# A two-layer decoder trunk on one core: c spread from a column, the compression MLP's matrices in long runs, the last sums ended in turn, and an order chosen with other durations

## The chip, the core and the metric

The kernel runs on one core of one Trainium2 chip. The metric is device time in microseconds (us), the median of several executions; a profiled execution of the same program shows where the time lies. The engines in the profile: PE is TensorE (matmuls; PEld its weight loads), DVE is VectorE, ACT is ScalarE, POOL is GpSimd, SP is SyncE, whose queue (SPq) issues nearly all loads. The engines work through their own instruction streams in order and wait for each other by semaphores.

## The reference, cut to what matters

```python
def reference(x, c, positions, w_ada, b_ada, norm_mix, norm_ffn, w_in, ...):
    cos, sin = rope_angles(positions)
    for l in range(DEPTH):
        ada = jax.nn.silu(c) @ w_ada[l] + b_ada[l]
        sh_m, sc_m, g_m, sh_f, sc_f, g_f = jnp.split(ada[:, None, :], 6, axis=-1)
        h = rms_norm(x, norm_mix[l]) * (1.0 + sc_m) + sh_m
        (q_a, kc_a, vc_a, ..., q_b, k_b, v_b, g_br) = jnp.split(h @ w_in[l], split_at, axis=-1)
        y_a = nsa_mixer(...)     # k_c = gelu(blocks(kc_a) @ ck_w1) @ ck_w2, likewise v_c
        y_b = moba_mixer(...)
        gate_a, gate_b = jnp.split(jax.nn.sigmoid(g_br), 2, axis=-1)
        merged = gate_a * (y_a @ w_up_nsa[l]) + gate_b * (y_b @ w_up_moba[l])
        x = x + g_m * (merged @ w_out[l])
        h = rms_norm(x, norm_ffn[l]) * (1.0 + sc_f) + sh_f
        gt, up = jnp.split(h @ w_ffn_in[l], 2, axis=-1)
        x = x + g_f * ((jax.nn.silu(gt) * up) @ w_ffn_out[l])
    return x
```

There are two layers, x is 256 tokens by 1024, c is one vector of 1024, and the hidden width of the second sublayer is 2816. All of it is float32. `nsa_cmp_k_w1` and `nsa_cmp_v_w1` (here ck_w1, cv_w1) are 2048 by 128.

## The kernel before

The 256 tokens are two tiles of 128 rows (t = 0, 1). A weight matrix is read once, in units of 1 MB (128 partitions by 2048 floats, a tile called raw; the first pass over w_in has units of 128 by 1816). To keep float32's precision at a faster matmul format, ACT rounds a unit to a tile hi, DVE forms lo = raw - hi, and PE does three matmuls for each product: hi with the activation's hi part, lo with it, and hi with the activation's lo part (hp holds both parts of h, hd is h before the split). A few units are multiplied as float32 straight from raw. There are three raw slots (and one spare), a few hi and lo slots, three slots aw for parts of w_ada, and eight banks for sums.

The kernel begins with a **lead**: x and c come in, silu(c) is spread over all partitions as crow (128 by 1024), and for each k of 8 the loads are a pair, sa (the shift and scale parts of w_ada, 1 MB) and raw (w_in). `ada_dot` (L707) multiplies sa by crow and sums each row on DVE; that gives the modulation of h for block k, without which hd and hp of that block, and so PE's matmuls on that unit, can't begin. In the lead POOL and ACT also work out the rotary tables (sincos, ct, st). c comes as a row of 1 by 1024 on SP's queue, ahead of x; two matmuls of a tile `ones` (1 by 128) with the row spread it.

After the lead comes the rest of w_in in units raw<-in_w_in. At its start stands the compression MLP (`mlp`, L1232), on the two matrices w1: each is loaded into a raw slot as 128 partitions by 16 pieces of 128 floats. Its 64 small matmuls need e, which DVE builds from the first products; `at` is ACT's copy of what they give, and two matmuls with `sel` follow. Further on are attention, w_up, w_out, then w_ffn_in and w_ffn_out (`sublayer_ffn`, L1538), and the second layer in the same way. Parts of w_ada for later use come in 0.5 MB pieces (aw) among the weight units, each with one ada_dot on DVE.

At the end, the last units of w_ffn_out end four sums (t, c), each a bank of 128 by 512. `gate` spreads g_f by eight transposes of gcol and two copies (gbc); `resid` (L1528) multiplies each bank by gbc and adds it to x on DVE, and SP stores the piece.

**What sets the order.** The code only records operations. `Program.order` (L246) then goes through them as a list scheduler with a duration for each operation, latencies between engines, and a model of the DMA queue, gives out slots and banks, and fixes each engine's stream. `levels` (L220) ranks operations by the longest path behind them; a `boost` is added to the rank. `fill` (L401) puts matmuls of zeros (zb) into PE's idle stretches longer than 1.4 us of the plan. `blame` and `rounds` (L421, L439) repeat the plan with other boosts and keep the shortest. So a changed duration can move any instruction on any engine.

Of the kernel before, what the change touches and what calls it, by code (L numbers as in the profile page):

```python
# [16 lines left out]
P = 128  # L17
# [107 lines left out]
LOOSE = {}  # L125
# [6 lines left out]
class Program:  # L132
    WAIT = 1.0

    FILL, IDLE, ZERO = 1.4, 1.0, 0.23
    FIRST_ZERO = (0.43, 11)

    ROUNDS, WEIGHT, START = 40, 1.0, 15.0
# [81 lines left out]
    def levels(self):  # L220
# [15 lines left out]
        for op in reversed(self.ops):  # L236
            c = min(c for c, _ in op.alts.values()) + (op.bytes / 385e3 + 2.0 if op.bytes else 0.0)
# [8 lines left out]
    def order(self):  # L246
# [17 lines left out]
        free = {e: 0.0 for e in LAT}  # L264
# [7 lines left out]

        def place(op):
            t = 0.0
            taken = {}
            picks = []
            if any(not v.placed for v in op.acc if v not in op.new):
                return None
            for v in op.new:
# [3 lines left out]
                if len(k.queue) <= i or k.queue[i] is not v:  # L283

                    if sum(not c.busy for s in k.slots for c in s.cells) - i <= LOOSE.get(v.name, 99):
                        return None
# [20 lines left out]
        while left:  # L307
            left -= 1
            best = None
            per = {}  # L310
            while loads and loads[0] in issued:
                loads.popleft()
            for op in ready:
# [5 lines left out]
                for e, (c, _) in op.alts.items():  # L319
# [4 lines left out]
                    per.setdefault(e, []).append((est, op, pl[1], c))  # L324
            self.done, self.ready = out, ready
            assert per, "stuck"
            for e, cs in per.items():
                t0 = min(c[0] for c in cs)
                if e == "SP":
                    pick = min(cs, key=lambda c: (max(c[0], free[e] + 0.3), c[1].no))  # L330
                else:
                    w = eps[e] + (self.SWITCH if e == "PE" else 0.0)
                    pick = max((c for c in cs if c[0] <= t0 + w), key=lambda c: (c[1].rank(e), -c[1].no))
                    if pick[3] > 1.0 and e != "PE":

                        soon = [c for c in cs if c[0] < t0 + self.WAIT * pick[3]
                                and c[1].rank(e) > pick[1].rank(e) + 5.0]
                        if soon:
                            pick = min(soon, key=lambda c: (c[0], -c[1].rank(e)))
                if best is None or pick[0] < best[0]:  # L340
                    best = (pick[0], e, pick[1], pick[2], pick[3])
            t, e, op, picks, c = best
            if len(op.alts) > 1:

                done = {x: next(y[0] for y in per[x] if y[1] is op) + op.alts[x][0] for x in op.alts}
                e = min(done, key=lambda x: done[x] + self.BIAS.get(x, 0.0))
                c = op.alts[e][0]
                t = done[e] - c
# [3 lines left out]
            for v, s in zip(op.new, picks):  # L352
                v.kind.queue.remove(v)
                v.slot, v.placed = s, True
                for cell in s.cells:
# [14 lines left out]
            if op.bytes:  # L370
                free[e] = t + c
                if e == "SP":
                    dma = max(dma, t + c + 0.5) + op.bytes / 385e3
                    end = dma + 2.0
                else:
                    end = t + c + 6.5
# [24 lines left out]
    def fill(self, t0, t1):  # L401
# [5 lines left out]
        cost, n = self.ZERO, int((t1 - t0 - self.IDLE) / self.ZERO)  # L407
        if t0 < 3.0:
            cost, n = self.FIRST_ZERO
# [29 lines left out]
    def rounds(self):  # L439

        best = None
        for i in range(self.ROUNDS):
# [4 lines left out]
            for op in self.ops:  # L447
                op.boost += self.WEIGHT * to.get(op.no, 0.0)
# [12 lines left out]
class Engines:  # L461
# [12 lines left out]
    def _vec(self, engs, n, two, fn, reads, writes, psum=False, extra=0.0):  # L474
        alts = {}
        for e in engs:
# [3 lines left out]
            else:  # L480
                alts[e] = (0.3 + n * (2.7e-3 if two else 2.0e-3) + extra, [lambda: fn(self.nc.gpsimd)])
# [89 lines left out]

SPILL = [("kb",), ("kb",)]
# [14 lines left out]
def trunk_kernel(tc, pools, A):  # L587
# [77 lines left out]
    ones = const("ones", [1, P])  # L665
# [302 lines left out]
    def consts():  # L968
# [5 lines left out]
        pool_memset(ones, 1.0, "DVE")  # L974
# [693 lines left out]
```

## Time and profile before

| | us |
|---|---|
| median of 3 runs | 835.67 (834.61 to 836.22) |
| the profiled execution, its own time | 833.42 |
| its span in the trace | 831.5 |
| PE busy | 810.5 (97%) |
| DVE busy | 578.0 (70%) |
| ACT busy | 419.9 (50%) |
| POOL busy | 66.1 (8%) |

The span runs from the first instruction to the end of the last, and 1.9 us of the execution's time lie outside it. Busy PE counts matmuls of zeros too. The granted clock over the span was 0.994 of the full one.

### The profile page before, as it was taken

To read this page: it belongs to the slowest core of one execution; us is meant where nothing else is said; L and a number is where in the kernel's file an instruction comes from. 1 tells how busy PE (TensorE), PEld (TensorE's weight loads), DVE (VectorE), ACT (ScalarE), POOL (GpSimd) and SP (SyncE) were. 2 spreads that over 40 slices of the span, in tenths; PEclk is the share of its full clock that TensorE was granted. 3 is DMA by queue.
4 is the path that set the end of the run, shared out by engine and by line. 5 is a ranking of instruction groups with operands and counts; after the bars stand their busy time and mean duration, and the time that the engine had idled before them with its cause. 6 is when DMAs were issued, how large, how long until landed. Compare 5 with 4: busy or idle time off the path is not lost.

```text
span 831.5 us, 10528 instructions
## 1 busy us (share of the span) xinstructions
PE 810.5 (97%) x3983; PEld 612.0 (74%) x3983; DVE 578.0 (70%) x1014; ACT 419.9 (50%) x667; POOL 66.1 (8%) x69
## 2 busy tenths in 40 slices
PE   9998999999999999999999999999999999999996
PEld 4566756764768887898878877776567888889885
DVE  6878877777787776778778897866378534464443
ACT  6444465861583433444376556587457534443331
POOL 4602610000000000000000313000000000000000
PEclk9999999999999999999999999999999999999999
DMA  9987474449938899887948775540284455465531
GB/s 364 381 302 254 135 263 134 178 158 333 343 121 298 281 304 327 303 308 287 347 153 283 248 239 183 187 151 1 102 294 162 138 189 181 151 203 202 200 104 50
DMA packets 75252, 183.82 MB, mean 221 GB/s; under 512 B 4129, under 2 KB 9265, under 8 KB 75202
## 3 DMA queue, kind: packets, MB, share of 16 engines
q1 hardware_dynamic: 75154, 183.08, 62.9%
q8 instruction: 31, 0.51, 0.3%
q14 instruction: 19, 0.16, 0.1%
q0 software_dynamic: 48, 0.08, 0.0%
HBM read 182.10 MB, written 1.05 MB: 220 GB/s over the span
## 4 chain that ended last, share of the span: by engine, by line
PE 77%; DVE 8%; DMA 8%; ACT 3%; issue 2%; POOL 2%; SPq 0%; DVEq 0%; POOLq 0%; ACTq 0%
PE bank L550 72%; PE bank L555 5%; DVE lo L485 4%; DMA aw<-in_w_ada 2%; DMA raw<-in_w_in 2%; ACT hi L533 2%; DMA rows<-in_rows 1%; DVE tmp L485 1%; DMA raw<-in_w_ffn_in 1%; DMA raw<-in_w_out 1%; POOL tmp L485 1%; DVE tmp L503 1%; POOL tmp L503 1%; DVE aw L491 1%; ACT hp L533 1%
## 5 line engine op out<-in xcount | busy, mean ns | idle before, releaser
L550 PE MATMUL bank<-hi,hp 128*128 128x512 f32 (+2 forms) x1296 | 408.8, 388 | 1.5 <-DVE hp L485 0.7
L485 DVE TENSOR_TENSOR lo<-raw,hi 128x2048 fp32r<-128x2048 f32 (+2 forms) x107 | 243.0, 2286 | 122.6 <-ACT hi L533 122.4
L533 ACT ACTIVATE hi<-raw 128x2048 fp32r<-128x2048 f32 (+2 forms) x107 | 201.7, 1892 | 230.3 <-PE bank L550 173.3
L550 PEld LDWEIGHTS bank<-hi,hp 128*128 128x128 f32 x1296 | 239.3, 189 | 57.0 <-issue 6.5
L550 PE MATMUL bank<-lo,hp 128*128 128x512 f32 (+2 forms) x648 | 244.9, 378 | 4.2 <-DVE lo L485 4.0
L550 PEld LDWEIGHTS bank<-lo,hp 128*128 128x128 f32 x648 | 122.4, 189 | 29.7 <-DVE lo L485 6.9
L491 DVE SCALAR_TENSOR_TENSOR aw<-aw,crow 128x1024 f32<-128x1024 f32 x80 | 95.8, 1219 | 24.6 <-DMA aw<-in_w_ada 24.4
L550 PE MATMUL bank<-hi,aT 128*128 128x512 f32 x352 | 111.9, 392 | 0.0
L550 PEld LDWEIGHTS bank<-hi,aT 128*128 128x128 f32 x352 | 66.1, 188 | 13.4
L550 PE MATMUL bank<-lo,aT 128*128 128x512 f32 x176 | 68.6, 390 | 0.0
L550 PE MATMUL bank<-raw,yy 128*128 128x512 f32 x128 | 58.3, 598 | 0.1
L550 PE MATMUL bank<-raw,hd 128*128 128x512 f32 (+1 forms) x112 | 49.1, 568 | 0.0
L550 PE MATMUL bank<-hi,mT 128*128 128x512 f32 x128 | 43.2, 404 | 0.1
L550 PEld LDWEIGHTS bank<-raw,yy 128*128 128x128 f32 x128 | 23.2, 190 | 26.2 <-issue 23.4
L497 DVE CUSTOM_DVE_ANT_0 at<-bank,maskf 128x128 f32<-128x128 f32 (+1 forms) x96 | 29.2, 352 | 16.6 <-PE bank L555 14.9
L555 PE MATMUL bank<-ident,tmp 128*128 128x128 f32 x256 | 38.6, 282 | 1.1 <-ACT tmp L874 0.4
L555 PEld LDWEIGHTS bank<-ident,tmp 128*128 128x128 f32 x256 | 31.3, 145 | 9.8 <-issue 2.6
L550 PEld LDWEIGHTS bank<-lo,aT 128*128 128x128 f32 x176 | 33.1, 188 | 6.3
L533 ACT ACTIVATE at<-at,nb,rqa 128x128 f32<-128x128 f32 (+1 forms) x64 | 34.2, 536 | 4.4 <-DVE nb L491 4.4
L550 PEld LDWEIGHTS bank<-raw,hd 128*128 128x128 f32 x112 | 20.3, 190 | 16.2 <-issue 14.3
L485 POOL TENSOR_TENSOR tmp<-tmp,tmp 128x512 f32<-128x512 f32 (+1 forms) x9 | 11.7, 1296 | 219.1 <-DVE tmp L491 212.6
L550 PEld LDWEIGHTS bank<-hi,mT 128*128 128x128 f32 x128 | 24.0, 188 | 5.7 <-DVE mT L491 0.6
(183 smaller groups left out, 723.5 us busy)
## 6 DMA issues: line engine op xcount, KB each, us to landing
raw<-in_w_ffn_in SPq DMA_DIRECT2D x44, 1024.0 KB, 5.9
aw<-in_w_ada SPq DMA_DIRECT2D x80, 512.0 KB, 4.8
raw<-in_w_in SPq DMA_DIRECT2D x30, 1024.0 KB, 5.1
raw<-in_w_ffn_out SPq DMA_DIRECT2D x22, 1024.0 KB, 5.2
sa<-in_w_ada SPq DMA_DIRECT2D x8, 1024.0 KB, 10.6
raw<-in_w_out SPq DMA_DIRECT2D x8, 1024.0 KB, 5.6
raw<-in_w_in SPq DMA_DIRECT2D x8, 908.0 KB, 8.5
raw<-in_w_up_nsa SPq DMA_DIRECT2D x4, 1024.0 KB, 5.3
```

What stands on the lines that cost most here:

```text
L485: self._vec(engs, cols(out), True, lambda v: v.tensor_tensor(AP(out), AP(a), AP(b), op=op), [a, b], [out])
L491: lambda v: v.scalar_tensor_tensor(AP(out), AP(a), AP(s), AP(b), op0=op0, op1=op1, **{k: AP(x) for k, x in kw.items()}),
L497: lambda v: v.tensor_tensor_reduce(AP(out), AP(a), AP(b), 1.0, init, op0, op1, AP(accum)),
L503: lambda v: v.tensor_scalar(AP(out), AP(a), AP(s1), AP(s2), op0=op0, **kw),
L533: op = self.p.op({"ACT": (c, [lambda: self.nc.scalar.activation(AP(out), AP(a), func, **{k: AP(x) for k, x in kw.items()})])}, reads + lis ...
L550: op = self.p.op({"PE": (cost, [lambda: self.nc.tensor.matmul(AP(out), AP(lhsT), AP(rhs), start=start, stop=stop)])}, [lhsT, rhs], [out])
L555: self.p.op({"PE": (0.109, [lambda: self.nc.tensor.transpose(AP(out), AP(a), AP(ident))])}, [a, ident], [out])
```

## The change

1. **c.** The host passes c as a column (128 by 8). ACT's own queue loads it, ahead of ACT's table load; tanh and the product are done on 128 by 8, and eight transposes of broadcast columns, four to a bank, with two copies make crow. `ones` and SP's load are gone.
2. **The first sa** comes in two DMAs of 0.5 MB, and each of its two dots waits for its own half.
3. **The MLP's w1** are put by the host into the layout of the tile, so that a partition reads one run of 2048 floats where it read 16 pieces of 128.
4. **The last sublayer's end.** The matmuls of the last three units are boosted so that the sums end in turn, the last sum is formed in two halves of 256 columns (36 matmuls where there were 18), and its product, addition and store go by halves. The gate's transposes are boosted.
5. **The planner** has other durations: DMA rate 412e3 bytes/us for 385e3, other DMA latencies, 0.43 us for an issue where it had 0.07, POOL slower, PE at double durations in the first 5.4 us, 60 rounds for 40 with fading boosts, slots given in strict order, and a choice of engine that counts what stands ahead on it.

```diff
@@ dma
-        eng = {"SP": self.nc.sync, "POOL": self.nc.gpsimd}[q]
-        self.p.op({q: (0.07 if q == "SP" else 0.6, [lambda: eng.dma_start(AP(out), AP(src))])},
-                  [src, *late], [out], nbytes=max(n, least))
+        n = max(n, least)
+        if o.shape[-1] < 1024:
+            n *= 1.07
+        eng = {"SP": self.nc.sync, "POOL": self.nc.gpsimd, "ACT": self.nc.scalar}[q]
+        self.p.op({q: ({"SP": 0.43, "ACT": 0.43, "POOL": 0.6}[q], [lambda: eng.dma_start(AP(out), AP(src))])},
+                  [src, *late], [out], nbytes=n)
@@ lead_in
-        cr = R.val("aw")[0:1]
-        dma(cr, A["c"])
+        cc = R.val("ccol")
+        dma(cc, A["c"], q="ACT")
...
-            dma(adas[k].rearrange("p (j c) -> p j c", j=2), src)
+            dst = adas[k].rearrange("p (j c) -> p j c", j=2)
+            for js in ((slice(0, 1), slice(1, 2)) if k < HALVED else (slice(0, 2),)):
+                dma(dst.of(js.start)[:, js] if k < HALVED else dst, src[:, js])
...
+        cg = R.val("ccol")
+        act(cg, cc, AF.Tanh, scale=0.5)
+        stt(cg, cg, 1.0, cc, ALU.add, ALU.mult)
         for i in range(2):
-            th = temp()
-            ci = cr[:, i * 512:(i + 1) * 512]
-            act(th[0:1], ci, AF.Tanh, scale=0.5)
-            stt(th[0:1], th[0:1], 1.0, ci, ALU.add, ALU.mult)
             b = R.val("acc")
-            mm(b, ones, th[0:1], True, True)
+            with R.burst():
+                for k in range(4):
+                    tr(b[:, k * P:(k + 1) * P], cg[:, 4 * i + k:4 * i + k + 1].to_broadcast([P, P]), ident)
             act(crow.of(i)[:, i * 512:(i + 1) * 512], b, AF.Copy)
@@ mlp
-                raw = R.val("raw").rearrange("p (j h) -> p j h", h=128)
-                dma(raw, A[f"nsa_cmp_{nm}_w1"][l].rearrange("(j p) h -> p j h", p=P))
-                w1.append(raw)
+                raw = R.val("raw")
+                dma(raw, A[f"nsa_cmp_{nm}_w1"][l])
+                w1.append(raw.rearrange("p (j h) -> p j h", h=128))
@@ sublayer_ffn
+        R.boost = 100.0 if l == L - 1 else 0.0
         gate(l, "g_f")
...
+            parts[(NT - 1, 1)] = [(0, 256), (256, 512)]
+            keys += [(i, t, k, c, e) for t in range(NT) for c in range(2) for e in parts[(t, c)]
+                     for i in range(nu - nl, nu) for k in range(2)]
...
+            R.boost = 20.0 * (4 - 2 * t - c) - e0 / 50 if l == L - 1 and i >= nu - nl else 0.0
+            mm3(b, aT[t][kk], us[i].hi[:, k, cs_], us[i].lo[:, k, cs_], kk == 0, kk == KF - 1 and e1 == 512)
...
+                for e0, e1 in parts[(t, c)]:
+                    xx = resid(l, t, c, bs[(t, c)], ada[l]["g_f"], e0, e1)
+                    dma(out[t * P:(t + 1) * P, c * 512 + e0:c * 512 + e1], xx)
@@ kernel (on the host)
+    for nm in "kv":
+        w = host[f"nsa_cmp_{nm}_w1"]
+        host[f"nsa_cmp_{nm}_w1"] = w.reshape(L, -1, P, w.shape[-1]).transpose(0, 2, 1, 3).reshape(L, P, -1)
```

**ACT in the lead**, at the rotary tables (sincos<-tmp), before:

```order
L533 ACTIVATE hp_302<-hd_300 128x256
L533 ACT_TABLE_LOAD
L533 ACTIVATE sincos_105<-tmp_76 128x96
L533 ACTIVATE tmp_76<-tmp_76 128x96
L533 ACTIVATE sincos_105<-tmp_76 128x96
L533 ACTIVATE hi_389<-raw_338 128x1816
L533 ACTIVATE hd_300<-pt_85,mod_m_136 128x256
L533 ACTIVATE hp_302<-hd_300 128x256
```

and in the changed kernel:

```order
L556 ACTIVATE hp_315<-hd_307 128x256
L556 ACT_TABLE_LOAD
L556 ACTIVATE sincos_106<-tmp_80 128x96
L556 ACTIVATE hi_392<-raw_339 128x1816
L556 ACTIVATE hd_307<-pt_85,mod_m_137 128x256
L556 ACTIVATE hp_315<-hd_307 128x256
L556 ACTIVATE tmp_80<-tmp_80 128x96
L556 ACTIVATE sincos_106<-tmp_80 128x96
```

The unit's hi, hd and hp moved ahead of the second sincos and of the step before it.

**SP's queue at the compression MLP** (raw<-in_nsa_cmp_k_w and _v_w are the two w1, the raw<-in_w_in behind them is the first unit of the rest of w_in), before:

```order
L563 DMA aw_72<-in_w_ada 128x1024
L563 DMA raw_522<-in_nsa_cmp_k_w 128x16x128
L563 DMA raw_528<-in_nsa_cmp_v_w 128x16x128
L563 DMA aw_73<-in_w_ada 128x1024
L563 DMA aw_74<-in_w_ada 128x1024
L563 DMA raw_555<-in_w_in 128x4x512
L563 DMA raw_677<-in_w_in 128x4x512
```

and in the changed kernel:

```order
L589 DMA aw_74<-in_w_ada 128x1024
L589 DMA raw_529<-in_nsa_cmp_k_w 128x2048
L589 DMA aw_72<-in_w_ada 128x1024
L589 DMA aw_73<-in_w_ada 128x1024
L589 DMA raw_555<-in_nsa_cmp_v_w 128x2048
L589 DMA raw_568<-in_w_in 128x4x512
L589 DMA aw_74<-in_w_ada 128x1024
L589 DMA raw_683<-in_w_in 128x4x512
```

The two aw moved ahead of the second w1, and a third aw now stands between the two units of w_in. On DVE its ada_dot stands ahead of the e builds, where before only two of these dots did.

**DVE at the end** (banks 63 to 67 hold the four sums), before:

```order
L485 TENSOR_TENSOR tmp_76<-bank_65,gbc_5786 128x512
L485 TENSOR_TENSOR tmp_79<-bank_67,gbc_5786 128x512
L485 TENSOR_TENSOR tmp_75<-bank_66,gbc_5786 128x512
L485 TENSOR_TENSOR tmp_77<-bank_63,gbc_5786 128x512
L485 TENSOR_TENSOR x_101<-x_101,tmp_76 128x512
L485 TENSOR_TENSOR x_101<-x_101,tmp_79 128x512
L485 TENSOR_TENSOR x_102<-x_102,tmp_75 128x512
L485 TENSOR_TENSOR x_102<-x_102,tmp_77 128x512
```

and in the changed kernel:

```order
L508 TENSOR_TENSOR tmp_80<-bank_63,gbc_5797 128x512
L508 TENSOR_TENSOR x_102<-x_102,tmp_80 128x512
L508 TENSOR_TENSOR tmp_78<-bank_67,gbc_5797 128x512
L508 TENSOR_TENSOR x_102<-x_102,tmp_78 128x512
L508 TENSOR_TENSOR tmp_76<-bank_66,gbc_5797 128x512
L508 TENSOR_TENSOR x_103<-x_103,tmp_76 128x512
L508 TENSOR_TENSOR tmp_77<-bank_64,gbc_5797 128x256
L508 TENSOR_TENSOR tmp_75<-bank_64,gbc_5797 128x256
L508 TENSOR_TENSOR x_103<-x_103,tmp_77 128x256
L508 TENSOR_TENSOR x_103<-x_103,tmp_75 128x256
```

Each product is now followed by its addition, and the last sum goes by halves. On PE the last unit's matmuls end bank 63, then 67, 66 and 64; ahead of them stand the eight transposes of gcol, which now all go to one bank (69), where before four went to bank 69 and four to 70.

## Rows read from the trace of the kernel before

**Rows 1.** Busy time of the engines in eight stretches: the stretch, its length, then PE, PEld, DVE, ACT and POOL busy (us, with instructions), PE's granted clock, the share of the DMA engines and GB/s.

```profile
0.00:13.56 13.56, 12.22 (x39) 5.92 (x40) 8.14 (x27) 9.90 (x19) 4.49 (x18) 0.87 0.86 336
30.50:33.40 2.90, 1.37 (x3) 0.37 (x2) 2.90 (x3) 0.42 (x1) 2.90 (x3) 1.00 0.67 263
33.40:61.30 27.90, 27.87 (x112) 19.02 (x113) 22.88 (x50) 12.97 (x26) 2.47 (x3) 1.00 0.91 321
61.30:64.80 3.50, 2.58 (x13) 1.01 (x11) 3.37 (x11) 0.60 (x1) 1.02 (x1) 1.00 1.03 399
67.30:71.50 4.20, 1.11 (x7) 1.04 (x7) 1.71 (x1) 3.17 (x6) 0.99 (x1) 0.90 0.79 257
71.50:74.10 2.60, 2.60 (x8) 1.89 (x7) 2.60 (x5) 2.17 (x3) 0.00 (x0) 0.51 1.05 399
74.10:820.87 746.77, 739.40 (x3666) 567.60 (x3664) 517.46 (x888) 381.68 (x599) 41.67 (x26) 1.00 0.61 211
824.90:831.50 6.60, 0.00 (x0) 0.00 (x0) 3.11 (x6) 0.00 (x0) 0.00 (x0) 0.76 0.42 159
```

**Rows 2.** The timeline of the lead's first 14 us: start, duration, engine (SPq is SP's queue), line, operation, out<-in, and in brackets the idle time before and what ended it.

```profile
0.73 0.35 SPq L563 DMA_DIRECT2D aw<-in_c  x1
...
1.13 0.83 SPq L563 DMA_DIRECT2D x<-in_x  x2
...
2.27 1.15 ACT L533 ACTIVATE tmp<-aw 1x512 f32<-1x512 f32 x2 [0.26 <-DMA aw<-in_c]
...
9.37 1.23 DVE L491 SCALAR_TENSOR_TENSOR sa<-sa,crow 128x1024 f32<-128x1024 f32 x1 [0.91 <-ACT crow L533]
...
12.23 0.60 ACT L533 ACTIVATE hd<-pt,mod_m 128x256 f32<-128x256 f32 x1 [0.18 <-DVE mod_m L485]
...
13.56 0.59 PE L550 MATMUL bank<-raw,hd 128*128 128x512 f32 x1
```

**Rows 3.** DMA issues of the first 20 us: out<-in, queue, operation, count, KB each, median us from issue to landing.

```profile
sa<-in_w_ada SPq DMA_DIRECT2D x4, 1024.0 KB, 10.5
...
vecs<-in_vecs POOLq DMA_DIRECT2D x1, 81.5 KB, 4.5
```

**Rows 4.** The timeline around 30 us, in the lead (columns as in Rows 2).

```profile
27.11 0.28 ACT L533 ACTIVATE sincos<-tmp 128x96 f32<-128x96 f32 x1 [2.03 <-POOL tmp L503]
...
28.29 1.71 ACT L533 ACTIVATE hi<-raw 128x1816 fp32r<-128x1816 f32 x1
...
30.03 2.48 DVE L485 TENSOR_TENSOR lo<-raw,hi 128x1816 fp32r<-128x1816 f32 x1 [2.67 <-ACT hi L533]
...
32.43 0.94 DVE L485 TENSOR_TENSOR hp<-hd,hp 128x256 fp32r<-128x256 f32 x1
...
33.43 0.74 PE L550 MATMUL bank<-hi,hp 128*128 128x512 f32 x2 [0.37 <-DVE hp L485]
```

**Rows 5.** The timeline of SP's queue at the compression MLP's loads (an issue's duration is the time until the queue has taken it).

```profile
51.42 0.83 SPq L563 DMA_DIRECT2D raw<-in_nsa_cmp_k_w  x1
52.70 1.67 SPq L563 DMA_DIRECT2D raw<-in_nsa_cmp_v_w  x1
54.41 3.99 SPq L563 DMA_DIRECT2D aw<-in_w_ada  x2
58.51 0.38 SPq L563 DMA_DIRECT2D raw<-in_w_in  x1
```

**Rows 6.** DMA issues from 50 to 64 us (columns as in Rows 3; the 0.5 KB of the w1 rows is one piece, the whole is 1 MB).

```profile
raw<-in_w_in SPq DMA_DIRECT2D x1, 1024.0 KB, 9.3
raw<-in_nsa_cmp_k_w SPq DMA_DIRECT2D x1, 0.5 KB, 6.6
raw<-in_nsa_cmp_v_w SPq DMA_DIRECT2D x1, 0.5 KB, 8.8
```

**Rows 7.** DMA issues of the whole span, from the page (columns as in Rows 3).

```profile
raw<-in_w_in SPq DMA_DIRECT2D x30, 1024.0 KB, 5.1
```

**Rows 8.** The timeline from the compression MLP to the first unit behind it (columns as in Rows 2).

```profile
64.86 0.23 PE L550 MATMUL bank<-zb,identb 128*128 128x128 bf16 x1 [0.98 <-DVE tmp L485]
...
65.02 1.98 PE L550 MATMUL bank<-raw,e 128*31 128x128 f32 x64
...
67.85 1.91 ACT L533 ACTIVATE hi<-raw 128x2048 fp32r<-128x2048 f32 x1 [5.65 <-DMA raw<-in_w_in]
...
69.79 2.29 DVE L485 TENSOR_TENSOR lo<-raw,hi 128x2048 fp32r<-128x2048 f32 x1 [2.93 <-ACT hi L533]
...
70.46 0.57 PE L550 MATMUL bank<-sel,at 128*128 128x60 f32 x2 [3.09 <-ACT at L533]
```

**Rows 9.** The timeline in layer 0's second sublayer, at an ada_dot (aw<-aw,crow) and the lo behind it on DVE.

```profile
316.07 1.22 DVE L491 SCALAR_TENSOR_TENSOR aw<-aw,crow 128x1024 f32<-128x1024 f32 x1 [5.67 <-DMA aw<-in_w_ada]
...
319.56 0.50 PE L550 MATMUL bank<-lo,hp 128*128 128x512 f32 x1 [1.50 <-DVE lo L485]
```

**Rows 10.** The timeline of the end (columns as in Rows 2).

```profile
821.73 1.09 ACT L542 ACTIVATE gbc<-bank 128x512 f32<-128x512 f32 x2 [8.18 <-PE bank L555]
...
822.92 2.68 DVE L485 TENSOR_TENSOR tmp<-bank,gbc 128x512 f32<-128x512 f32 x4 [8.09 <-PE bank L550]
...
825.52 2.48 DVE L485 TENSOR_TENSOR x<-x,tmp 128x512 f32<-128x512 f32 x4
826.23 2.14 SPq L563 DMA_DIRECT2D out<-x  x4
```

More of the change, by code (lines that the diff above doesn't have):

```diff
@@ L236, in levels @@
         for op in reversed(self.ops):
-            c = min(c for c, _ in op.alts.values()) + (op.bytes / 385e3 + 2.0 if op.bytes else 0.0)
+            c = min(c for c, _ in op.alts.values()) + (op.bytes / 412e3 + 1.8 if op.bytes else 0.0)
             e = next(iter(op.alts))
@@ L263, in order @@
         rt = {op.no: {} for op in self.ops}
-        free = {e: 0.0 for e in LAT}
+        free = {e: 0.7 for e in LAT}
         dma = 0.0
@@ L271, in order @@
         parts = False
+        parked, aside = {}, set()
         def place(op):
             t = 0.0
+            picks = []
+            for v in op.acc:
+                if not v.placed and v not in op.new:
+                    parked.setdefault(id(v), []).append(op)
+                    aside.add(op)
+                    return None
+            if not op.new:
+                return t, picks
             taken = {}
-            picks = []
-            if any(not v.placed for v in op.acc if v not in op.new):
-                return None
             for v in op.new:
@@ L282, in place @@
                 taken[id(k)] = i + 1
-                if len(k.queue) <= i or k.queue[i] is not v:
-                    if sum(not c.busy for s in k.slots for c in s.cells) - i <= LOOSE.get(v.name, 99):
-                        return None
+                if k.queue[i] is not v:
+                    if i == 0:
+                        parked.setdefault(id(v), []).append(op)
+                        aside.add(op)
+                    return None
                 best = None
@@ L309, in order @@
             best = None
-            per = {}
+            per, first = {}, {}
             while loads and loads[0] in issued:
                 loads.popleft()
+            aside.clear()
             for op in ready:
@@ L324, in order @@
                     per.setdefault(e, []).append((est, op, pl[1], c))
+            if aside:
+                ready = [op for op in ready if op not in aside]
             self.done, self.ready = out, ready
@@ L342, in order @@
             t, e, op, picks, c = best
+            if e == "PE" and t < self.COLD:
+                c = c * 2
             if len(op.alts) > 1:
-                done = {x: next(y[0] for y in per[x] if y[1] is op) + op.alts[x][0] for x in op.alts}
+                done = {x: max(next(y[0] for y in per[x] if y[1] is op),
+                               0.0 if first[x][1] is op else first[x][0] + first[x][3]) + op.alts[x][0] for x in op.alts}
                 e = min(done, key=lambda x: done[x] + self.BIAS.get(x, 0.0))
-                c = op.alts[e][0]
-                t = done[e] - c
+                if first[e][1] is not op:
+                    t, op, picks, c = first[e]
+                    if len(op.alts) > 1:
+                        c = op.alts[e][0]
+                else:
+                    c = op.alts[e][0]
+                    t = done[e] - c
             op.waits = [(f if q == e else f + LAT[q], self.ops[n]) for n, (f, q) in rt[op.no].items()]
@@ L352, in order @@
             for v, s in zip(op.new, picks):
-                v.kind.queue.remove(v)
+                v.kind.queue.popleft()
                 v.slot, v.placed = s, True
+                ready += parked.pop(id(v), ())
+                if v.kind.queue:
+                    ready += parked.pop(id(v.kind.queue[0]), ())
                 for cell in s.cells:
@@ L372, in order @@
                 if e == "SP":
-                    dma = max(dma, t + c + 0.5) + op.bytes / 385e3
-                    end = dma + 2.0
+                    dma = max(dma, t + c + 0.1) + op.bytes / 412e3
+                    end = dma + 1.75
                 else:
-                    end = t + c + 6.5
+                    end = t + c + (2.0 if e == "ACT" else 4.0)
             else:
@@ L441, in rounds @@
         best = None
+        own = [op.boost for op in self.ops]
         for i in range(self.ROUNDS):
@@ L664, in trunk_kernel @@
     sel = const("sel", [P, 60])
-    ones = const("ones", [1, P])
+    tiles("ccol", 2, [P, KD])
     mhalf = const("mhalf", [P, 1])
```

60 lines of the change are left out of this document (34 added, 26 removed).

## The prediction

> **What bounds the kernel now.** I read the busy time by stretches first. From 74.1 us to 820.87 us PE is busy for 739.40 of 746.77 us at the full granted clock [rows 1], so PE bounds the kernel, and 7.4 us there is all that a better order could take back. The change gives PE about the same work (the same products, the last sum in more pieces). So the time can fall only where PE idles, runs zeros or runs slowly: before the first real matmul at 13.56 us, where most of its 12.22 busy us are zeros; at 30.5 to 33.4 us, 1.5 us idle; around the compression MLP, where 61.3 to 64.8 is nearly all zeros, 67.3 to 71.5 has 3.1 us idle and the next 2.6 us run at a granted clock of 0.51, the lower level; in those 7.4 us; and after PE's last matmul, 6.6 us [rows 1]. The timelines then tell what ends each wait.
>
> **The lead (parts 1 and 2).** c is SP's first issue, and x follows 0.40 us behind it [rows 2]; with c on ACT's queue, all loads behind it come 0.40 us sooner. Three chains then matter.
> First, crow: before, two tanh on one partition take 1.15 us, and crow's second half releases the first dot at 9.37 us [rows 2]. As a column, tanh and product have 8 elements a partition, and eight transposes stand for two matmuls. If the column lands about as the row did (it released ACT at 2.27 us), crow is there some 3 us sooner, and then the dot waits for sa. sa takes 10.5 us from issue to landing in the median of this stretch; the first was issued early and its dot shows no wait for it, so it is in by 9.37 us. Its first half may be in a microsecond before that. So the first real matmul comes 1 to 2 us sooner, but the second unit needs its own sa and raw, and those win only the 0.40 us of the queue. I take -0.6 us there.
> Second, at 30 us, ACT works off the sincos steps from 27.11 on and begins hi at 28.29; lo runs until 32.51, hp follows it on DVE, and PE waits until 33.43 [rows 4]. In the new order hi stands directly behind the first sincos, so about 0.9 us earlier (28.29 less 27.39), and PE's 1.5 idle us shrink by that or more. Together some -1.9 us at 33 us.
> Third, the loads of the lead stream at the DMA's rate, so at its end something between the queue's 0.4 and the full 1.9 us is left. I take **-1.5 us** at 59 us (0.6 to 1.9). The tables that are pushed back on ACT are needed only after the lead; their cover is the work until 59 us. I cost them at nothing, up to 0.6 us if it fails.
>
> **The compression MLP (part 3).** Before, PE stands behind two chains. One is DVE's rope and e work, which releases the 64 small matmuls at 65.02 (64.86 is the wait's end) [rows 8]. The other is the load of the first w_in unit behind the MLP: issued at 58.51 [rows 5], 9.3 us to landing [rows 6], hi on ACT at 67.85 after 5.65 idle us, `at` behind hi on ACT, and PE's sel matmuls at 70.46 after 3.09 idle us [rows 8]; lo ends at 72.08. The unit is late because the first w1 takes 6.6 us and the second 8.8 [rows 6], where a w_in unit takes 5.1 in the median [rows 7], and SP is held in the issues of the second w1 and the aw behind it for 1.67 and 3.99 us [rows 5].
> In the change the same 4.2 MB (two w1, two aw, the unit) go through from some 50 us. At the 399 GB/s of 61.3 to 64.8 us [rows 1] that is 10.5 us, and with some 2 us of start and end (5.1 us for 1 MB, of which 2.6 at that rate are transfer) the unit lands near 62.5 to 63. That is 5 us earlier, and more than can be used, since DVE's chain is next: 64.86 less the lead's 1.5, plus one ada_dot of 1.22 us (the price in [rows 9]) that the new order puts ahead of the e builds, gives 64.6. The small matmuls take 1.98 us [rows 8], `at` no longer waits behind hi, and lo can begin when DVE has done the rest of its ropes, about 66.4, and end at 68.7 where it ended at 72.08. That is -3.4 us, the lead's 1.5 in it. PE's idle time before it becomes short, so I expect the granted clock to stay at its upper level; of the 1.3 us that the 2.6 us at 0.51 cost, some 0.5 lay in the wait for lo anyway, which leaves -0.8. Lead and MLP together: **-4.2 us** (-2 to -5.5). The second layer's w1 lie beside dense work; nothing there.
>
> A rule of the Trainium skill speaks against this part. The trace shows 512-byte pieces landing 1.5 us later than 8 KB runs do [rows 6, 7]. The Trainium skill, "DMA: Bandwidth & Descriptors", section "Specifications", puts the smallest transfer at line rate at 512 B, by which the old pieces were already at full rate and the new layout would win nothing; the sum would then be that of the first rival below.
>
> **The end (part 4).** Before, the four products take 2.68 us from 822.92 on and the four additions follow from 825.52 to 828.00 [rows 10], 3.1 us behind PE's end at 824.9 [rows 1]; all four sums end within PE's last 3 us. In the change each product is followed by its addition and keeps pace with PE: a sum's last six matmuls are some 1.36 us, a product and an addition 0.67 + 0.62 [rows 10]. Behind PE's end stand at most two half products and two half additions, 1.3 us: -1.8 us. Against it: all eight gate transposes go to one bank, so four wait for the first copy of 0.55 us [rows 10] and the hand-over, about +0.9, with nothing but the last sums queued behind them on PE. And 18 more matmuls: from nothing to 18 x 31 ns (64 small ones in 1.98 us [rows 8]), 0.6; I take +0.2, as they stream the same columns in all. Sum **-0.7 us** (-2.3 to +0.2).
>
> **The order (part 5)** moves instructions everywhere. The 7.4 idle us after 74.1 us [rows 1] are some dozen waits, mostly for lo, the longest 1.50 us [rows 9]. At the second layer's start the new order puts a lo later (+0.5), elsewhere waits should go, as the planner now reckons with the issue times of 0.4 us that the trace shows [rows 5]. I take **-0.6 us** (-4 to +4).
>
> Sum: -4.2 - 0.7 - 0.6 = -5.5 us. The profiled execution's 833.42 becomes 827.9; it lies 2.25 us under the median of 835.67, so the forecast is **830.2 us**.
>
> **The rivals.**
> 1. *The long runs are hidden.* If 512-byte pieces cost nothing themselves, and the w1 rows are long only because the queue is full, the w_in unit lands with the lead's gain alone, about 1 us earlier, and the idle time before 71.5 and the dip of the clock recur. For it: the two w1 are in flight together from 52.70 to 58.0 [rows 5, 6], so a part of their length is sharing. Against it: a second transfer doesn't slow the first in a queue that works in order, and the rate of 399 GB/s comes in the stretch that begins as the second w1 has landed (52.70 + 8.8 = 61.5), with 321 in the one before [rows 1]. Then -1.0 - 0.7 - 0.6 = -2.3: 833.4.
> 2. *Slower: dots ahead of lo.* On DVE an ada_dot whose aw is late holds up the lo behind it: 5.67 us idle before the dot, then 1.50 us of PE waiting [rows 9]. The new order has more such places, with several dots ahead of a lo and only three aw slots. Each costs about 1.5 us on PE if its aw lands later than the plan's 1.75 us behind the transfer. Three take back the 4.5 us of lead, MLP and end less the rest; six cost 9, so 835.67 - 4.9 + 9 = 839.8. Against it: DVE has 30% slack, and its ready times are planned with a DMA nearer to the trace.
> 3. *The order wins more.* If the new durations remove most of the 7.4 us, -5 in place of -0.6: 825.8. Waits for lo behind ACT and DVE are of the sort that a better model sees. Against it: each place is its own.
> 4. *c comes late.* Pieces of 32 bytes, 128 partitions: if the column takes as long as vecs, 4.5 us [rows 3], from 0.7, it is there at 5.2 and still before the first sa, so nothing changes. It decides only beyond some 7 us, and then 1 us for 1: about 835.
>
> **How the numbers follow.** The forecast has 52% (828 to 832.4), rival 1 15%, rival 2 9%, rival 3 20%, rival 4 4%. A measurement of this kernel tells about 0.2%, 1.7 us, from no change. Faster by more than that is under 834.0: the forecast, rival 3 and most of rival 1, 82%. Within it: the rest of rival 1, rival 4 and the mildest of 2, 10%. Slower 8%. The range for 8 in 10 reaches into rival 3 and over rival 1: 824.4 to 834.6.
>
> **What would show it.** The first real matmul before 12.6 us and no wait over 1 us near 30 us (lead). The first w1 landing in 5 to 5.5 us, ACT's hi on the first w_in unit before 64 us, lo ending near 68.7, the granted clock full from 67 to 74 us (MLP). A span that ends 4.8 us behind the last matmul, and some 0.9 us of PE waiting for a gbc copy (end). PE idle after the MLP of 6 to 7.5 us. Wrong it would be if PE waits for lo behind dots at several new places, or if the w_in unit lands early and the small matmuls still begin at 65 us or later, because DVE has become the bound there.

## The result, and the profile after

The changed kernel takes 841.52 us (median of 7, 837.77 to 844.84) against 834.81 us (median of 7) before: 1.008 times as long, 95% interval 1.0054 to 1.0106. It is slower by some 0.8%, where 5.5 us less (0.7%) was forecast. The profiled execution is one of 840.15 us, with a span of 838.3 us, 6.8 us longer than before.

Where the 6.8 us lie is told by busy time over stretches that end at the same events: the first real matmul, the two sel matmuls of layer 0, the first matmul of layer 0's second sublayer and the end of that sublayer, the first attention matmul of layer 1, the first matmul of its second sublayer, PE's last matmul. Before (columns as in [rows 1]):

```profile
13.56:70.46 56.90, 51.28 (x249) 32.45 (x247) 43.66 (x89) 24.48 (x43) 19.89 (x25) 1.00 0.90 338
70.46:235.20 164.74, 163.51 (x791) 109.27 (x791) 129.83 (x308) 91.55 (x192) 21.05 (x14) 0.99 0.63 217
235.20:428.90 193.70, 191.04 (x912) 157.92 (x912) 147.74 (x171) 87.74 (x89) 0.00 (x0) 1.00 0.81 286
428.90:483.54 54.64, 52.87 (x319) 42.69 (x318) 46.73 (x85) 32.76 (x55) 7.31 (x4) 1.00 0.75 250
483.54:636.20 152.66, 151.13 (x778) 106.99 (x778) 106.67 (x258) 94.21 (x194) 13.31 (x8) 1.00 0.48 162
636.20:824.90 188.70, 188.49 (x901) 156.73 (x899) 92.10 (x79) 79.23 (x77) 0.00 (x0) 1.00 0.45 156
```

and after:

```profile
0.00:13.32 13.32, 10.66 (x44) 5.86 (x44) 6.35 (x25) 7.11 (x14) 5.81 (x18) 1.00 0.88 344
13.32:68.02 54.70, 50.72 (x246) 32.33 (x246) 45.68 (x91) 26.13 (x47) 22.67 (x25) 1.00 0.94 356
68.02:234.68 166.66, 164.18 (x791) 109.26 (x792) 135.87 (x317) 90.42 (x188) 21.57 (x18) 0.99 0.67 235
234.68:435.30 200.62, 193.43 (x911) 159.87 (x909) 148.47 (x176) 87.39 (x89) 0.00 (x0) 0.98 0.79 276
435.30:492.99 57.69, 55.24 (x326) 43.43 (x325) 48.56 (x87) 32.18 (x56) 9.36 (x6) 1.00 0.67 229
492.99:644.00 151.01, 150.82 (x779) 106.60 (x778) 100.22 (x245) 91.76 (x191) 12.30 (x7) 1.00 0.42 143
644.00:833.87 189.87, 188.96 (x920) 157.78 (x918) 93.78 (x82) 78.73 (x77) 0.00 (x0) 1.00 0.45 157
833.87:838.30 4.43, 0.00 (x0) 0.00 (x0) 1.42 (x5) 0.00 (x0) 0.00 (x0) 1.00 0.40 143
```

Read the first number behind each stretch. Up to the sel matmuls the change wins 2.4 us (68.02 for 70.46), and behind PE's last matmul 2.2 us (4.43 for 6.60 in [rows 1]). Between the two it loses 11.4 us: 1.9, then **6.9 in layer 0's second sublayer**, 3.1 at the start of layer 1, -1.7 and 1.2. In the sublayer PE's work is nearly the same (193.43 and 191.04 us busy), its idle time grew from 2.7 to 7.2 us, and the granted clock is 0.98 over the stretch.

**The sublayer.** The timeline at its first long wait, after:

```profile
271.57 6.00 ACT L556 ACTIVATE hi<-raw 128x2048 fp32r<-128x2048 f32 x3 [10.32 <-PE bank L573]
...
273.72 1.23 DVE L514 SCALAR_TENSOR_TENSOR aw<-aw,crow 128x1024 f32<-128x1024 f32 x1 [6.03 <-DMA aw<-in_w_ada]
...
276.19 1.22 DVE L514 SCALAR_TENSOR_TENSOR aw<-aw,crow 128x1024 f32<-128x1024 f32 x1
...
277.34 4.49 DVE L508 TENSOR_TENSOR lo<-raw,hi 128x2048 fp32r<-128x2048 f32 x2
...
279.68 0.79 PE L573 MATMUL bank<-lo,hp 128*128 128x512 f32 x1 [2.96 <-DVE lo L508]
```

This is [rows 9] again, longer. The first hi is done at 273.5, so lo could begin. But DVE's stream has three dots ahead of it, the first of which has waited 6.03 us for its aw; lo begins 3.8 us later, at 277.34, and PE waits 2.96 us. Two such places follow (2.07 us at 339.75, 1.37 us at 383.22). The two longer waits cost twice, since the granted clock fell to half, its lower level, behind them (columns as in [rows 1]):

```profile
279.70:282.70 3.00, 3.00 (x7) 2.42 (x8) 3.00 (x2) 0.00 (x0) 0.00 (x0) 0.50 0.99 366
340.70:344.20 3.50, 3.50 (x11) 2.70 (x10) 3.50 (x3) 0.00 (x0) 0.00 (x0) 0.51 0.87 266
```

Some 3.2 of these 6.5 us are lost. Behind the wait of 1.37 us the granted clock stayed at 1.00 (383.2 to 390 us). Before, there was one such long wait in the stretch, 1.50 us, and the clock stayed at 1.00 behind it too. The number of dots is not what differs: 43 lie in the stretch after and 41 before.

The loads there also take longer than in the kernel before. From 235 to 390 us, before (columns as in [rows 3]):

```profile
raw<-in_w_ffn_in SPq DMA_DIRECT2D x17, 1024.0 KB, 6.1
aw<-in_w_ada SPq DMA_DIRECT2D x34, 512.0 KB, 4.6
```

and after:

```profile
aw<-in_w_ada SPq DMA_DIRECT2D x42, 512.0 KB, 5.1
raw<-in_w_ffn_in SPq DMA_DIRECT2D x16, 1024.0 KB, 7.1
```

By the durations in the diff the plan reckons with 3.55 us for a piece that finds the queue empty (0.43 + 0.1 + 0.524 MB at 412 GB/s + 1.75), and with 5.0 us for a unit (1.049 MB, with the factor 1.07). These are also the medians that the planner of the changed kernel itself works out for that stretch; the planner of before works out 4.1 and 5.3. So the plan of before was 0.5 and 0.8 us too early, and that of the changed kernel 1.5 and 2.1.

**The lead**, after; compare [rows 2, 4]:

```profile
4.41 0.21 ACT L556 ACTIVATE ccol<-ccol 128x8 f32<-128x8 f32 x1 [1.97 <-DMA ccol<-in_c]
...
8.31 1.22 DVE L514 SCALAR_TENSOR_TENSOR sa<-sa,crow 128x1024 f32<-128x1024 f32 x1
...
9.98 1.34 ACT L901 ACTIVATE tmp<-x,rx 128x512 f32<-128x512 f32 x2 [1.23 <-POOL rx L887]
...
11.40 1.91 PE L578 MATMUL bank<-ident,tmp 128*128 128x128 f32 x16
...
13.32 1.36 PE L573 MATMUL bank<-raw,hd 128*128 128x512 f32 x3
```

The column lands 2.1 us later than the row did (4.41 for 2.27), and the first dot begins 1.06 us sooner, with no wait for crow or sa in its row. But the first real matmul wins only 0.24 us: x's second tile is now scaled behind the crow copies, its transposes begin at 11.40, and hd comes behind them. The wait at 30 us shrank as forecast: hi begins at 27.53, and PE waits 0.36 us at 31.37 where it had 1.08 and 0.37; a wait of 0.68 us for hd came in at 36.12.

**The MLP**, after; compare [rows 6, 8]:

```profile
raw<-in_nsa_cmp_k_w SPq DMA_DIRECT2D x1, 1024.0 KB, 4.9
raw<-in_nsa_cmp_v_w SPq DMA_DIRECT2D x1, 1024.0 KB, 8.0
raw<-in_w_in SPq DMA_DIRECT2D x1, 1024.0 KB, 9.7
```

```profile
63.20 1.98 PE L573 MATMUL bank<-raw,e 128*31 128x128 f32 x64
...
65.41 1.91 ACT L556 ACTIVATE hi<-raw 128x2048 fp32r<-128x2048 f32 x1 [4.99 <-DMA raw<-in_w_in]
...
68.02 0.69 PE L573 MATMUL bank<-sel,at 128*128 128x60 f32 x2 [2.46 <-ACT at L556]
```

The first w1 takes 1.7 us less. The unit still lands only at 65.4. Two aw that wait for their slots now stand ahead of the second w1, which is issued at 54.19; in run 2 below, whose order is that of before, it is issued at 51.62 and the unit lands at 63.9. So PE again waits for `at` behind hi, and the clock dips again (0.50 in 67.70 to 71.10).

**The end**, after; compare [rows 10]:

```profile
827.64 0.65 PE L578 MATMUL bank<-ident,gcol 128*128 128x128 f32 x4 [0.69 <-ACT gbc L565]
...
833.87 0.76 DVE L508 TENSOR_TENSOR tmp<-bank,gbc 128x256 f32<-128x256 f32 x2
834.54 0.75 DVE L508 TENSOR_TENSOR x<-x,tmp 128x256 f32<-128x256 f32 x2
```

Only half a product pair and half an addition pair stand behind the last matmul, and four gate transposes wait 0.69 us for the copy of their bank.

### The profile page after: what moved, and what is told of

Same layout as the page of the kernel before. It is cut to its first block, busy times and chain, and to the rows that moved or that the text cites. A ratio compares the mean times of both kernels' runs of the same rounds, so it can differ in the third digit from the quotient of the medians.

```text
span 838.3 us, 10577 instructions
## 1 busy us (share of the span) xinstructions
PE 814.0 (97%) x4008; PEld 615.1 (73%) x4008; DVE 580.4 (69%) x1023; ACT 413.7 (49%) x657; POOL 71.7 (9%) x74
## 5 line engine op out<-in xcount | busy, mean ns | idle before, releaser
L573 PE MATMUL bank<-lo,hp 128*128 128x512 f32 (+1 forms) x648 | 246.2, 380 | 7.2 <-DVE lo L508 7.1
L573 PE MATMUL bank<-hi,aT 128*128 128x512 f32 (+1 forms) x364 | 111.8, 385 | 0.0
L573 PE MATMUL bank<-lo,aT 128*128 128x512 f32 (+1 forms) x182 | 69.9, 384 | 1.4 <-DVE lo L508 1.4
L865 POOL TENSOR_TENSOR r<-r,mhalf 128x4 f32<-128x4 f32 x4 | 5.1, 1273 | 360.5 <-DVE r L526 360.4
```

What stands on the lines that cost most here:

```text
L573: op = self.p.op({"PE": (cost, [lambda: self.nc.tensor.matmul(AP(out), AP(lhsT), AP(rhs), start=start, stop=stop)])}, [lhsT, rhs], [out])
L865: E_.raw("POOL", 1.1 + 0.13 * n, lambda: nc.gpsimd.tensor_tensor(AP(r), AP(r), AP(mh), op=ALU.pow), [r, mhalf], [r])
```

## The experiments

Times are medians; the ratio is to the kernel before, run on the same chip in the same rounds (its medians were 834.85 to 835.93 us). The changed kernel had 1.008 in the rounds of the result; it was not run again, so differences to it in us go by medians of other rounds.

**1. Dots behind lo at three places** (the changed kernel's order kept, eight dots moved).

```diff
-        for t, e, op in self.rounds():
+        for t, e, op in turned(self, self.rounds(), TURNS):
```

Here `turned` moves the named dots, and the loads into the aw slots that they free, behind the lo's that follow. The eight dots are those of the first and of the third long wait (2.96 and 1.37 us), and those at 353.7 to 359.5 us, where PE waited only 0.17 us. The two dots of the second long wait (2.07 us) are not among them, so this run and run 7 leave that place as it was, unlike what their expectations say.

> The changed kernel with its order kept but for three places in layer 0's second sublayer, where eight ada_dots are put behind the lo's that follow them on DVE (with the loads that wait for those dots). Theory, dots ahead of lo: PE's waits of 2.96, 2.07 and 1.37 us for lo go, and with the first two the dips of the granted clock; 5 to 8 us less than the changed kernel's 841.5, about 834 to 837. Rival, the loads themselves are late there, whatever DVE does first: within 1.5 us of the changed kernel.

Measured 846.72 us, 1.0128 (1.0107 to 1.0149): 5 us worse, outside both ranges. The first wait went (PE waits for no lo between 250 and 300 us). But the aw loads that were moved stood ahead of weight loads on SP's queue, which works in order:

```profile
277.06 0.38 SPq L589 DMA_DIRECT2D raw<-in_w_ffn_in  x1
282.60 2.62 SPq L589 DMA_DIRECT2D aw<-in_w_ada  x3
285.32 4.54 SPq L589 DMA_DIRECT2D raw<-in_w_ffn_in  x3
```

SP stood from 277.4 to 282.6 at an aw load that waited for a moved dot, three weight units were issued in a row behind it, and the next aw behind those, from 290.63 on. The first of these took some 10 us to land, and its dot and two more stood ahead of the next lo:

```profile
295.44 6.00 ACT L556 ACTIVATE hi<-raw 128x2048 fp32r<-128x2048 f32 x3 [10.31 <-PE bank L573]
...
300.73 1.23 DVE L514 SCALAR_TENSOR_TENSOR aw<-aw,crow 128x1024 f32<-128x1024 f32 x1 [7.83 <-DMA aw<-in_w_ada]
...
306.69 0.79 PE L573 MATMUL bank<-lo,hp 128*128 128x512 f32 x1 [6.09 <-DVE lo L508]
```

The first hi was done at 297.4, and lo began at 304.35. So the wait of 6.09 us is again one for a lo behind dots, at a place that the edit did not touch, and the edit had made its aw later. Neither theory had this: a dot's place on DVE also sets when the loads behind its slot are issued. The second long wait came again too (2.58 us at 345.74).

**2. The long runs alone** (kernel before, its order unchanged).

```diff
-                raw = R.val("raw").rearrange("p (j h) -> p j h", h=128)
-                dma(raw, A[f"nsa_cmp_{nm}_w1"][l].rearrange("(j p) h -> p j h", p=P))
-                w1.append(raw)
+                raw = R.val("raw")
+                dma(raw, A[f"nsa_cmp_{nm}_w1"][l])
+                w1.append(raw.rearrange("p (j h) -> p j h", h=128))
```

> The kernel before, order and all, with only the layout of the two w1 changed to runs of 8 KB. Theory: the first w1 lands in 5.1 us where it took 6.6, the first w_in unit behind the MLP at about 64 where it landed at 67.8, and the small matmuls still begin at about 65 since DVE bounds them; 2 to 3.5 us less than before, about 832. Rival, 512-byte pieces cost nothing and the queue was full anyway: within 0.7 us of before.

Measured 833.41 us, 0.9969 (0.9954 to 0.9985), 2.6 us less. Its timeline at the unit behind the MLP:

```profile
63.88 1.92 ACT L533 ACTIVATE hi<-raw 128x2048 fp32r<-128x2048 f32 x1 [1.88 <-DMA raw<-in_w_in]
64.67 0.23 PE L550 MATMUL bank<-zb,identb 128*128 128x128 bf16 x1 [0.99 <-DVE tmp L485]
...
67.21 0.43 PE L550 MATMUL bank<-sel,at 128*128 128x60 f32 x2
```

The unit lands 4 us sooner, the sel matmuls come 3.25 us sooner, and the small matmuls stay where DVE's chain puts them (64.83), as forecast. The loads (columns as in [rows 6]):

```profile
raw<-in_nsa_cmp_k_w SPq DMA_DIRECT2D x1, 1024.0 KB, 4.7
```

While the w1 came in, the DMA engines moved 401 GB/s (53 to 58 us) where they had moved 293 before (55 to 60 us), and they were busy in both. The granted clock stayed at 1.00 from 67.3 to 76 us, though PE waited 2.40 us at 70.05, for POOL.

**3 and 4. One planner setting each put back**: WAIT in run 3, the DMA in run 4.

```diff
-    WAIT = 0.5
+    WAIT = 1.0
...
-                    dma = max(dma, t + c + 0.1) + op.bytes / 412e3
-                    end = dma + 1.75
+                    dma = max(dma, t + c + 0.5) + op.bytes / 385e3
+                    end = dma + 2.0
```

> The changed kernel with the planner's WAIT at 1.0 as before (an engine holds back for a higher-ranked instruction up to that multiple of the duration of the one it could begin), all else as changed. If the halved WAIT is what let the dots go ahead of lo: fewer waits for lo in layer 0's second sublayer, 834 to 838. If it is the faster DMA of the plan: 839 to 843, with the waits for lo still there.

> The changed kernel with the planner's old DMA rate and latency (385e3 bytes/us, 0.5 and 2.0 us; the new issue time of 0.43 us kept). If the faster DMA of the plan is what let the dots go ahead of lo: the plan puts the dots later, waits for lo fall, 832 to 837. If it is the halved WAIT or the new boosts: 839 to 843.

Measured 836.99 us, 1.0019 (1.0002 to 1.0036), and 837.89 us, 1.0023 (1.0006 to 1.0041). Each alone takes back about 4 us of the 6.7, so neither is the one cause. Run 3 lies in its first range, run 4 between its two. In both traces waits for lo are left in layer 0's second sublayer, but the longest is 1.58 and 1.51 us where it was 2.96, and the granted clock there is 1.00. Run 3 has 46 dots in that sublayer, more than the changed kernel, and still loses less.

**5 and 6. The edits without the planner, the planner without the edits.** Run 5 has the whole class Program of the kernel before and its durations of issues and of POOL; run 6 has those of the changed kernel in the kernel before. Of run 5, against the changed kernel:

```diff
-    WAIT = 0.5
+    WAIT = 1.0
...
-    ROUNDS, WEIGHT, FADE, START = 60, 1.0, 0.95, 15.0
+    ROUNDS, WEIGHT, START = 40, 1.0, 15.0
...
-                    dma = max(dma, t + c + 0.1) + op.bytes / 412e3
-                    end = dma + 1.75
+                    dma = max(dma, t + c + 0.5) + op.bytes / 385e3
+                    end = dma + 2.0
```

> Parts 1 to 4 of the change with the planner of before (its class, its DMA and issue durations). Theory, the edits bring what the two traces show for lead, MLP and end (2.7 + 2 us) and the new planner loses more than that: 829 to 833. Rival, the edits themselves disturb the order, whoever plans it: 836 to 842.

> The kernel before with the new planner alone (part 5: class, durations, issue times), no part 1 to 4. Theory, the new planner is what loses: 840 to 846, with waits for lo of 1 to 3 us in layer 0's second sublayer. Rival, it loses only together with the edits: 833 to 838.

Measured 833.42 us, 0.9979 (0.996 to 0.9999), and 847.31 us, 1.0151 (1.0123 to 1.0179). The planner alone costs some 12 us, and the edits, with the old planner, bring some 2. Both lie just outside the range of the theory, on the side of less gain and more loss. PE's waits for lo over the whole span (total us, times, longest), in the changed kernel and in run 6:

```profile
PE bank L573 <- DVE lo L508: 8.5, 7, 3.0
PE bank L573 <- DVE lo L508: 10.9, 11, 2.6
```

In layer 0's second sublayer run 6 has three long ones, of 2.03, 2.65 and 2.42 us.

**7. Dots behind lo, and the weights ahead of the aw loads** (`move` is what run 1 does).

```diff
+    for dots, los, more in turns:
+        loads = move(dots, los)
+        at = max(i for i, (_, _, op) in enumerate(out) if op.no in loads)
+        raws = [op.no for _, e, op in out[at:] if e == "SP" and any(v.name == "raw" for v in op.new)][:more]
+        move(loads, raws)
```

> The changed kernel with its order kept, the eight ada_dots put behind the lo's at the same three places as before, and now also the aw loads that follow from them put behind the next one or two weight units on SP's queue, so that no weight load stands behind an aw load that waits for a moved dot. Theory, the dots ahead of lo cost the waits and the earlier try lost through SP's queue alone: 834 to 838. Rival, the waits move on to the next units in any order, since loads and slots have no slack there: 840 or more.

Measured 842.58 us, 1.0077 (1.0055 to 1.0099): no better than the changed kernel, in the rival's range. The wait at 280 us went, and this one came:

```profile
297.24 6.00 ACT L556 ACTIVATE hi<-raw 128x2048 fp32r<-128x2048 f32 x3 [10.32 <-PE bank L573]
...
298.79 1.23 DVE L514 SCALAR_TENSOR_TENSOR aw<-aw,crow 128x1024 f32<-128x1024 f32 x1 [3.89 <-DMA aw<-in_w_ada]
...
303.07 4.49 DVE L508 TENSOR_TENSOR lo<-raw,hi 128x2048 fp32r<-128x2048 f32 x2
...
305.41 0.50 PE L573 MATMUL bank<-lo,hp 128*128 128x512 f32 x1 [3.02 <-DVE lo L508]
```

The rival was right that the waits move on. But the weights were not late here: hi is done at 299.2, and lo begins at 303.07 behind dots of the next group, whose aw were now late in their turn. It is the same mechanism at the next place, as in run 1. And the second long wait, whose dots were not moved, is still there:

```profile
339.26 1.23 DVE L514 SCALAR_TENSOR_TENSOR aw<-aw,crow 128x1024 f32<-128x1024 f32 x1 [5.28 <-DMA aw<-in_w_ada]
...
343.99 0.50 PE L573 MATMUL bank<-lo,hp 128*128 128x512 f32 x1 [2.25 <-DVE lo L508]
```

So runs 1 and 7 can't decide for or against the theory; "in any order" is answered by runs 9 and 11, which change the rule at all places.

**8. Both settings back** (the two edits of runs 3 and 4 together).

> The changed kernel with both WAIT at 1.0 and the planner's old DMA rate and latency. If each of the two settings takes back its own part of the loss: 831 to 835. If any new plan has its own waits, whichever setting is used: 835 to 840, no better than either alone.

Measured 834.69 us, 0.9987 (0.9975 to 0.9999): in the range of the first, and better than either alone.

**9. Dots give way everywhere.**

```diff
-    WAIT = 0.5
+    WAIT = 2.5
```

> The changed kernel with the planner's WAIT at 2.5 in place of 0.5, so that in the plan DVE holds a dot of 1.2 us back whenever a lo can begin within 3 us; the faster DMA of the plan stays. Theory, dots ahead of a lo that is soon due are what loses, at every such place: below the 837.0 of WAIT at 1.0, 832 to 836. Rival, beyond a little holding back the order of dots and lo's doesn't matter, the plan's DMA does: 837 to 841.

Measured 833.05 us, 0.9969 (0.995 to 0.9988), 8.5 us under the changed kernel, with the plan's fast DMA kept; it lies in the first range. In the sublayer one wait for lo is left, 1.15 us.

**10. The dots without their loads** in layer 0's second sublayer.

```diff
-            for f in op.alts[e][1]:
+            for f in () if e == "SP" and 243.0 < t < 360.0 and op.new and op.new[0].name == "aw" else op.alts[e][1]:
```

> The changed kernel with its order kept, and the 36 loads of w_ada pieces (aw) in layer 0's second sublayer left out, so that their dots work on what the slot held and wait for no load; the dots themselves stay, and the output is not the reference's. Theory, late aw hold the dots and the dots hold the lo's: the waits for lo between 240 and 390 us go, 832 to 836. Rival, DVE has too much to do there or hi comes too late, whatever the loads do: 839 to 842. Leaving out 18 MB of transfers also makes the weight units land sooner, so a gain doesn't tell the two ways of a load's lateness apart.

Measured 831.4 us, 0.9942 (0.9917 to 0.9968), a little below the theory's range. With the same order and the same work on DVE, no wait for lo is left between 240 and 390 us. PE's waits for lo over the whole span (columns as in run 6), all of them elsewhere:

```profile
PE bank L573 <- DVE lo L508: 2.6, 4, 0.8
```

So DVE's work alone does not make the waits; the loads do. Whether by the late aw or by the units that the aw delay, this run can't tell; the row at 273.72 above, where the unit's hi was done and the dot still had to wait for its aw, and run 11 speak for the aw.

**11. The plan told that aw come late.**

```diff
-                    end = dma + 1.75
+                    end = dma + (4.25 if op.new and op.new[0].name == "aw" else 1.75)
```

> The changed kernel whose plan lets an aw load land 2.5 us later than now (4.25 in place of 1.75 us behind its transfer), nearer to the 4.4 to 8.4 us from issue to landing in layer 0's second sublayer; weight units as in the changed plan. Theory, the plan's early aw is what puts dots ahead of lo's: 833 to 837. Rival, the weight units' planned landing is what is wrong: 838 to 842.

Measured **831.96 us, 0.9946 (0.9926 to 0.9966)**: by the medians 2.9 us under the kernel before and 9.6 under the changed one, the best of the versions that compute the whole, and below the theory's range. Its second sublayer of layer 0, in the columns of [rows 1]:

```profile
234.00:428.00 194.00, 193.82 (x932) 160.96 (x930) 143.40 (x167) 90.11 (x95) 0.00 (x0) 1.00 0.76 274
```

PE idles 0.2 us of 194, at the full clock, and units of w_ffn_in land in 5.3 us in the median where the changed kernel had 7.1. Its aw take 5.5 us, which is less than the plan now reckons with. Its order differs in more than that, though: 37 dots are left in the stretch.

**12. Long runs and the end, with the planner of before** (parts 3 and 4 of the change alone; besides the lines of run 2, against the kernel before):

```diff
+        R.boost = 100.0 if l == L - 1 else 0.0
         gate(l, "g_f")
...
+            parts[(NT - 1, 1)] = [(0, 256), (256, 512)]
...
+            R.boost = 20.0 * (4 - 2 * t - c) - e0 / 50 if l == L - 1 and i >= nu - nl else 0.0
```

> The kernel before and its planner with parts 3 and 4 alone (long runs, the end in turn and in halves), c and the first sa as before. If the end brings the 1.5 us that the trace of the changed kernel shows, beside the 2.6 of the runs: 830 to 832.5. If the end's gain is used up by the gate's wait, the halves and a moved order: 832.5 to 834.5.

Measured 834.52 us, 0.9983 (0.9961 to 1.0005), which is not told apart from the kernel before nor from run 2. It lies at the upper edge of the second range; that the end brings anything in time is not shown by it.

## Why the prediction was wrong

The step that failed is the last term: "The order (part 5) ... I take -0.6 us (-4 to +4)". Runs 5 and 6 part the planner from the edits: the planner costs 11.6 us alone and 8.1 on top of the edits (841.5 for 833.4), two to three times the upper bound. I read the 7.4 idle us after 74 us as what a better model of the DMA could take back, and bounded the loss at 4 us. The trace of before had the case that says otherwise [rows 9], and I put it among the rivals at 9%, with the right mechanism and the right place; waits for lo behind dots were also the first sign that I named for being wrong. The price of a place was too low, since I missed the clock: three places cost 2.96, 2.07 and 1.37 us of waiting and some 3.2 us at the lower level, about as much as the rival put on six. Its weight was low because the planned DMA was "nearer to the trace". It was nearer to the rate of a full queue (412 GB/s planned, 399 in 61.3 to 64.8 us [rows 1]). In layer 0's second sublayer the median aw took 1.5 us longer than in the plan, and the median unit 2.1.

A second cause stands neither in the list of the change nor in the prediction: the change also halves the planner's WAIT, from 1.0 to 0.5, so that DVE holds a dot back for a lo only half as long. The old planner's slower DMA and longer hold-back had been margin, and the change took both: runs 3, 4 and 8 put them back one by one and together (837.0, 837.9, 834.7), run 9 restores the margin by the hold-back alone (833.1), run 11 by the loads' time alone (832.0), and run 10 shows that without the loads the same order has no such waits. One rival is not fully excluded: each of these plans but run 10 is a new order, and the changed kernel's could have been an unlucky one of many. Against it, the same settings lost in run 6 too, where the program is another, and five plans with one or the other margin all lost less. No run made a new plan with the settings left alone.

The other steps, by the same order:

- **The lead**: -0.24 at the first matmul where 1 to 2 us were forecast, since the order put x's second tile behind crow; the wait at 30 us went from 1.45 to 0.36 us, as taken. The small matmuls of the MLP, which DVE's chain releases, begin 1.8 us sooner (63.20 for 65.02), and not at 64.6: the dot that I added 1.22 us for ended at 57.6 us, before the e builds began at 59.36. (It is the dot of an earlier aw; the third aw takes its slot.)
- **The MLP**: right in kind and shown apart by run 2 (-2.6 us; the sel matmuls 3.25 us sooner). The first w1 took 6.6 us in pieces of 512 bytes and 4.7 to 4.9 in 8 KB runs. The Trainium skill ("DMA: Bandwidth & Descriptors", section "Specifications") puts the smallest transfer at line rate at 512 B; here the measurement decides against it. One reading in the prediction was wrong: the w_in units of [rows 7] are four pieces of 2 KB a partition (128x4x512 in SP's queue), so their 5.1 us is not that of 8 KB runs; run 2 gives that. Off in size: in the changed kernel the unit landed at 65.4 and not at 63, with the second w1 issued behind two aw, and the dip of the clock that I took as gone came back. -2.7 us at the first attention matmul (76.64 for 79.35) stand for the -4.2.
- **The end**: -2.2 us behind PE's last matmul (-1.8 forecast), against 0.69 us of waiting for the gbc copy (0.9 forecast); the last stretch before it is 1.2 us longer. Net about -1.0 in the trace, forecast -0.7. Runs 5 and 12 don't show it in time.
- **The second layer's start** cost 3.1 us where +0.5 was taken: seven zeros (1.67 us) and 0.69 us stand before a lo where 0.96 us stood, and another wait for a lo, of 0.84 us, comes later.

Also open is why the planner alone (847.3) loses more than planner and edits together (841.5), where the edits with the old planner bring only 2. Every plan differs from the next in thousands of places, and a few us between two plans were not traced to single ones.

## What to carry to other kernels

When a schedule is made against a model, the durations that matter are not the best that a transfer reaches but those it has where the plan uses them. A model that is made faster, without the loads becoming so, takes margin away just where two engines meet. Before an optional instruction is put ahead of one that the bound engine waits for, ask when its input lands at the latest, and what else its delay will hold: here a dot held a lo, and in run 1 a load that waited for a dot held the weights behind it on an in-order queue. A few waits seen in a trace are better mended in the rule that makes them than one by one, as the wait goes to the next place of the kind.

## What was not expected

- A column of 128 pieces of 32 bytes, 4 KB in all, took 3.7 us from issue to landing on ACT's queue at the start, and the tanh began 2.1 us later than on the row (4.41 for 2.27).
- Moving eight dots and their loads cost 5 us more (run 1): one waiting load on SP's queue held three weight units for 5.2 us, these made the next aw late, and their dots held the next lo.
- The changed kernel's seven times spread by 7.1 us, those of before by 3.3. That says nothing of the change: in the rounds of the experiments the kernel before spread by 7.4 to 8.4 us over 23 to 31 executions.
